# Experts of layer 1 take their tokens by one-hot products on the chip instead of gathers and transposes

## The chip, the cores and the metric

The kernel runs on one core of a Trainium2 chip. A run is one launch; its time is the device time in microseconds (us). The time of the kernel before is the median of three runs.

## The reference

Two layers of a hybrid backbone. Each layer mixes tokens (attention and a convolution), and then sends every token through the two best of 16 experts (a mixture of experts, MoE). Layer 0 does this for 512 tokens (256 of the context and 256 of the stream), layer 1 for the 256 of the stream. What matters here is the MoE; `t` has 1024 columns, an expert's inner width is 512, all in f32:

```python
combine = jnp.sum(jax.nn.one_hot(idx, N_EXPERTS) * wsel[..., None], axis=1)
y = jnp.zeros_like(t)
for e in range(N_EXPERTS):
    he = jax.nn.silu(t @ wg[e]) * (t @ wu[e])
    y = y + combine[:, e:e + 1] * (he @ wd[e])
```

`combine` is zero but for the two experts of a token, so a kernel need compute for each expert only the tokens that chose it. The product of a 0/1 matrix with the rows `t` that picks those tokens is exact in f32.

## The kernel before, in words

**The experts.** The expert's three matrices come as six tiles of 1 MB (two of `wg`, two of `wu`, two of `wd`) through a ring of 17 tiles. The SP queue issues them (L230), a tile as soon as one of the ring is free. All products of the experts run on TensorE (PE), in an order written out by hand in `moe`: in the iteration of expert e come the first halves of gate and up (`widen`, 32 matmuls), then the tokens of expert e+1 (`turn_tokens`), the transposes of the inner activations of expert e-1 (`turn_inner`), the second halves of gate and up (32 matmuls, for a wide expert 32 more of `widen_rest`), and the down product of e-1 (`down`, 48 matmuls, or `down_narrow`, 32). In layer 1 experts 0 to 5 are wide (96 places for tokens), 6 to 15 narrow (64 places).

**The tokens.** The normed and modulated rows `h` go to an array in device memory, `h2d`, 128 rows at a time (L841, on the SP queue). After routing, DVE builds a one-hot tile of the places of an expert, PE multiplies it with a table (`slots`, L1064: three columns that give the row numbers, three that give the weights), DVE turns the product into row numbers (`find`) and weights (`weigh`). With the row numbers POOL issues an indirect load (`gather`, L954) of 96 or 64 rows of 4 KB from `h2d`. The rows lie with tokens on the partitions, so PE transposes them in eight pieces (`turn_tokens`, L1214), and ACT and DVE copy the result `gp` into `tx`, the stationary operand of gate and up. The first two experts are found and gathered right after routing, each later one two iterations ahead.

**The opening of layer 1.** Around 700 us the order of the engines comes from generators that are woven together. `ada_row` makes the modulation rows: 64 products `ada` on PE, and then an add on DVE of a bias tile `ab`, which POOL's queue loads (L404); on POOL's queue these loads stand in program order between the loads (L2013) and the adds (L2039) of the filter spectra `K`. The list `held` holds the bias tiles that were asked for ahead; its entry 0 is that of the first row.

**The last experts.** Three experts at the end (TAIL) are added by products on the chip; the rest of a token's output is fetched by indirect loads into row buffers (`others_rows`).

Of the kernel before, what the change touches and what calls it, by code (L numbers as in the profile page):

```python
# [14 lines left out]
F32 = mybir.dt.float32  # L15
# [3 lines left out]
AF = mybir.ActivationFunctionType  # L19
ALU = mybir.AluOpType  # L20
# [4 lines left out]
P = 128  # L25
D = 1024
KD = 8
EPS = 1e-6
NEG = -1e30
NE = 16  # L30
# [219 lines left out]
def tile_hybrid_flow(ctx, tc, xin, rows, adab, w_ada, w_in_e, w_out_e, sinkb, rpb, w_in_o, w_out_o, hyw,  # L250
# [28 lines left out]
    def tpt(name):  # L279
        return btile([P, 4, P], "tp", name)  # L280
# [27 lines left out]
    def cc(name):  # L308
        o, n = CONST_AT[name]
        return cst[:, o : o + n]  # L310
# [510 lines left out]
    def g_h2(l, i, ti, a, h2, g2, sh2, rss, how):  # L821

        ss = small.tile([P, 1], F32, name=f"ssm{l}_{i}", tag="ss", bufs=4)
        S.activation(h2, xrow(ti), AF.Square, accum_out=ss)
        S.activation(rss[i], ss, AF.Sqrt, bias=epsc, scale=1.0 / D)
        yield
        V.reciprocal(rss[i], rss[i])

        def scale():
            V.scalar_tensor_tensor(h2, xrow(ti), rss[i], g2[:, a], op0=ALU.mult, op1=ALU.mult)  # L830

        if how in ("early", "first"):
            scale()
        yield
        if how == "late":
            scale()
        elif how == "aside":
            S.activation(h2, xrow(ti), AF.Copy, scale=rss[i])
            G.tensor_mul(h2, h2, g2[:, a])
        (V if how == "first" else G).tensor_add(h2, h2, sh2[:, a])  # L840
        SY.dma_start(h2d[l][i * P : (i + 1) * P, :], h2)  # L841
        yield
        yield

# [112 lines left out]
    def slot_table(l, pool):  # L957

        NT = 4 if l == 0 else 2
        tab = pool.tile([P, NT, NE, 6], BF, name=f"tab{l}")  # L960
        tb3 = tok_b.rearrange("p (i a) -> p i a", a=2)[:, 0:NT]
        for a in range(2):
            G.tensor_copy(tab[:, :, :, a], tb3[:, :, a : a + 1].to_broadcast([P, NT, NE]))
        G.tensor_copy(tab[:, :, :, 2:3], cc("far").unsqueeze(1).unsqueeze(2).to_broadcast([P, NT, NE, 1]))
        return tab

    def g_route(l, pool, s, r):
# [81 lines left out]
        def find(src, n, idst, hp):  # L1049

            f = hp.tile([P, NE], F32, name=f"idf{l}", tag="idf", bufs=1)[:, 0:n]
            V.reduce_sum(f, src[:, :, 0:3], axis=AX.X)
            newest["slots"] = V.tensor_scalar_add(idst, f, 4096.0).ins
# [4 lines left out]
        def slots(es, parts, idp=None):  # L1058
            idp = tpt(f"ids{l}_{es[0]}")[:, 0] if idp is None else idp
            for e in es:  # L1060
                for i in range(NT):
                    hot = one_hot(pool, lambda i: posm[:, i * NE + e : i * NE + e + 1], 0, i, 4, e >= WIDE[l])
                    o = 6 * (e - es[0])
                    T.matmul(idp[:, o + parts.start : o + parts.stop], hot, tab[:, i, e, parts], start=(i == 0), stop=(i == NT - 1))  # L1064
            return idp[:, 0 : 6 * len(es)].rearrange("p (e a) -> p e a", a=6)

        for e in range(2):
            find(slots([e], slice(0, 3)), 1, ids[:, e : e + 1], pool)
            gather(l, r["gts"][e][0 : SLOTS[l]], ids[0 : SLOTS[l], e : e + 1])
        if l == 0:  # L1070
# [47 lines left out]

        def group(e, idp):

            idp = slots([e], slice(0, 6), idp)
            at = slice(e, e + 1)

            def rest():
                find(idp, 1, ids[:, at], pool)
                weigh(idp, csl[:, at])

            return rest
# [39 lines left out]
            idp = slots([0, 1], slice(3, 6), idp)  # L1168
            return lambda: weigh(idp, csl[:, 0:2])

        r.update(eids=eids, weigh_first=weigh_first, posm=posm, ids=ids, csl=csl, group=group, rest=rest, find=find, weigh=weigh, one_hot=one_hot, pos=pos)
        yield

    def slots_hot(hot, at):
# [21 lines left out]
    def moe(l, r, gate5):  # L1196
# [7 lines left out]
        lp = lctx.__enter__()  # L1204
        def slots_of(e):
            return N if e < WIDE[l] else NARROW

        def turn_tokens(e):

# [145 lines left out]

        def others_rows(i):

            if i:
                t = W.pools["rest"][0].tile([P, 2, D], F32, name="yr0", tag="wt") if l == 0 else keep.tile([P, 2, D], F32, name="yr1", tag="xr0")
                d = [t[:, 0], t[:, 1]]  # L1360
            else:
                d = gts
            ex["rows", i] = combine_get(l, d, yb[0 : row_at(l, NE - TAIL[l]) + 1, :], r["rowi"], NT - 2 + i)

        def others_add(e, i):
# [36 lines left out]
            skip_runtime_bounds_check_because="a place's number is a sum over a one-hot row of the numbers of the experts")  # L1402
        lined = tc.manual_schedule(engines={T.engine})
        lined.__enter__()
        tx = turn_tokens(0)
        for e in range(NE + 1):
            if e:
                he = inner(e - 1, gu)
            if e < NE:
                gu = [acc(f"gu{l}_{e}_{a}") for a in range(1 + (e < WIDE[l]))]  # L1410
                cur, ups = tx, []
                widen(e, cur, gu, ups, 0)
            if e in (NE - 2, NE - 1):
                others_rows(NE - 1 - e)
            if e + 1 < NE:
                tx = turn_tokens(e + 1)
            if e:
                hx = turn_inner(e - 1, he)
            if e == NE - 2:
                others_slots()  # L1420
            if e == NE:
                for i in (1, 0):
                    others_take(i)
                others_open()
            if l and e == NE - 1:
                r["fg"] = W.pools["rest"][0].tile([P, 2, D], F32, name="fg", tag="wt")[:, 0]
                SY.dma_start(r["fg"], final_g[0].partition_broadcast(P))
            if e < NE:
                widen(e, cur, gu, ups, 1)
            if e:  # L1430
                (down if e <= WIDE[l] else down_narrow)(e - 1, hx)
            if e < WIDE[l]:
                widen_rest(cur, gu, ups)
            if e == NE - 1:
                W.limit = len(specs)
            if e == 1:
                with tc.issue_after(newest[V]):
                    r["rest"]()
# [569 lines left out]
    def hy_load(o):  # L2008
        K = [[None] * 2, [None] * 2]
        for ci in range(2):  # L2010
            for ft in range(2):
                K[ci][ft] = pool.tile([P, 512], F32, name=f"K{o}{ci}{ft}", tag="K", bufs=4)
                G.dma_start(K[ci][ft], kspec[o, ci, ft * P : ft * P + P, :])  # L2013
        return K
# [65 lines left out]
    def tail_side():  # L2080
# [4 lines left out]
        yield  # L2085
        yield from g_hyf(1, Ks[1])

    Ks = {0: hy_load(0)}
    weave(g_hyf(0, Ks[0]), chain(dense, ada_row(0)), 1.2)
    next_pools = {}  # L2090
# [31 lines left out]
    g2 = bcast(1, 4, pg, (1,))  # L2122
    sh2 = bcast(1, 3, pg, (1,))
    route1 = {}
    rows1 = m1.tile([P, 3, D], F32, name="rows1", tag="h2parts")
    G.memset(rows1[:, 0:2], 0.0)
    lgT = ypt("lg1")
    rss = [pb.tile([P, 1], F32, name=f"rsm1_{i}") for i in range(2)]
    rw = []
# [1 line left out]
    next(shares)  # L2131
    gate5 = bcast(1, 5, pb, (1,))
    h2x = keep.tile([P, 2, D], F32, name="h2x", tag="xr0")
    route1.update(gts=[rows1[:, 0], rows1[:, 1]], third=rows1[:, 2], tab=slot_table(1, pb))
    s1 = route_in(1, pg, pb, ob[1], shares, rw, [(2 + i, 1, 0) for i in range(2)], g2, sh2, rss, lgT, None, lambda i: h2x[:, i])
    routing = g_route(1, pb, s1, route1)
    next(routing)
# [65 lines left out]
```

## Time and profile before

| what | value |
|---|---|
| median of three runs | 1163.7 us (1157.68, 1163.7, 1164.82) |
| the profiled execution's own time | 1155.26 us |
| its span in the profile | 1153.1 us |
| PE busy | 1002.1 us, 87% of the span |
| DVE, ACT, POOL busy | 555.7, 382.2, 144.7 us |
| granted TensorE clock, mean of the span | 0.947 |
| moved by DMA | 328.88 MB, mean 285 GB/s |

The span is the stretch between the first and the last recorded instruction; 2.2 us of the execution's time lie around it. A clock of 1.00 is 2.4 GHz, 0.50 is 1.2 GHz. A busy PE is one that has a matmul in flight, and a time between the starts of two matmuls (their pitch) is what one costs in a row of them; the durations shown beside them overlap. "Landing" is the time from the issue of a transfer to its end.

### The profile page before, as it was taken

What the parts mean: (1) busy time and instruction counts of PE and PEld (TensorE: products, weight loads), DVE (VectorE), ACT (ScalarE), POOL (GpSimd) and SP (SyncE); (2) the same over time, 40 slices, a digit from 0 to 9 for tenths busy, and PEclk for the clock granted to TensorE, in tenths of its full rate; (3) what the DMA queues carried; (4) which work ended last, traced back from release to release, by engine and by line L of the source; (5) the groups of instructions that cost most, each with busy time, mean ns of one, the idle gap of its engine ahead of it and who ended that gap; (6) DMA issues with size and microseconds to landing.
All of it is one profiled execution on the core that took longest, in us unless ns stands there. A gap on an engine that the chain in (4) does not pass through costs nothing. (4 is left out here: it accounts for less than half of the span.)

```text
span 1153.1 us, 20964 instructions
## 1 busy us (share of the span) xinstructions
PE 1002.1 (87%) x8420; PEld 554.9 (48%) x8420; DVE 555.7 (48%) x1398; ACT 382.2 (33%) x855; POOL 144.7 (13%) x170
## 2 busy tenths in 40 slices
PE   5899999889893899999998677968893999998975
PEld 3587877566672333333332476767661333332222
DVE  7664655566447532332312683467656434321114
ACT  4545444342322233333221461443332333211111
POOL 2320002210205100000001102222012000000010
PEclk9999999999996899999999888998995999999997
DMA  8942122892957999999999835445288899999993
GB/s 332 420 142 75 37 74 71 311 331 79 404 222 272 320 323 388 405 398 395 402 400 420 342 130 229 147 151 190 91 354 300 280 368 413 403 383 409 418 418 162
DMA packets 55693, 328.88 MB, mean 285 GB/s; under 512 B 8546, under 2 KB 9026, under 8 KB 21474
## 3 DMA queue, kind: packets, MB, share of 16 engines
q1 hardware_dynamic: 41043, 285.93, 63.4%
q0 software_dynamic: 10096, 29.70, 7.8%
q10 hardware_dynamic: 4448, 11.81, 2.8%
q8 instruction: 70, 1.15, 0.4%
q14 instruction: 36, 0.29, 0.1%
HBM read 315.54 MB, written 16.06 MB: 288 GB/s over the span
## 5 line engine op out<-in xcount | busy, mean ns | idle before, releaser
L1234 PE MATMUL gu<-wt,tx 128*32 128x512 f32 x2560 | 305.5, 605 | 19.8 <-DMA wt<-in_moe_wu_dram 17.4
L1234 PEld LDWEIGHTS gu<-wt,tx 128*32 128x32 f32 x2560 | 81.8, 111 | 211.0 <-issue 170.9
L1234 PE MATMUL y<-wt,hx 128*32 128x512 f32 x1280 | 147.4, 593 | 0.0
L1234 PEld LDWEIGHTS y<-wt,hx 128*32 128x32 f32 x1280 | 43.8, 110 | 95.2 <-issue 93.2
L515 DVE TENSOR_TENSOR pair<-wt,pair 128x512 fp32r<-128x512 f32 x104 | 68.9, 711 | 16.6 <-ACT pair L512 16.4
L1223 ACT ACTIVATE tx<-gp 128x192 f32<-128x192 f32 (+1 forms) x64 | 19.3, 304 | 151.9 <-PE gp L1214 124.5
L1265 DVE TENSOR_TENSOR yo<-yo,y 32x512 f32<-32x512 f32 x32 | 21.8, 683 | 90.9 <-ACT yo L1263 90.6
L512 ACT ACTIVATE pair<-wt 128x512 fp32r<-128x512 f32 x104 | 58.4, 625 | 14.7 <-DMA wt<-in_w_in_o_dram 11.5
L1275 DVE TENSOR_TENSOR he<-he,up 96x512 f32<-96x512 f32 (+1 forms) x32 | 21.9, 685 | 82.4 <-ACT up L1274 81.9
L1224 DVE COPY tx<-gp 128x192 f32<-128x192 f32 (+1 forms) x64 | 20.3, 322 | 79.0 <-ACT tx L1223 78.5
L1270 ACT ACTIVATE he<-gu 96x512 f32<-96x512 f32 (+1 forms) x32 | 18.9, 591 | 116.2 <-PE gu L1234 116.2
L429 PE MATMUL ada<-wt,siluT 128*32 128x128 f32 x1536 | 51.3, 282 | 3.7 <-ACT pt L770 2.0
L429 PEld LDWEIGHTS ada<-wt,siluT 128*32 128x32 f32 x1536 | 41.5, 113 | 15.3 <-issue 8.1
L954 POOL DMA_INDIRECT gt<-h2d,ids x16 | 15.6, 976 | 202.8 <-DVE hot L1176 92.2
L1265 DVE TENSOR_TENSOR up<-up,gu 32x512 f32<-32x512 f32 x32 | 21.8, 683 | 36.3 <-ACT up L1263 36.0
L954 POOL DMA_INDIRECT rows<-h2d,ids x16 | 15.3, 958 | 182.7 <-DVE hot L1176 95.0
L768 PE MATMUL tp<-ident,pr 128*128 128x128 f32 x256 | 33.9, 275 | 0.0
L757 DVE TENSOR_SCALAR pr<-pr,ls 128x512 f32<-128x512 f32 (+1 forms) x80 | 32.5, 457 | 1.1
L741 ACT ACTIVATE pr<-sB,ng 128x512 f32<-128x512 f32 (+1 forms) x32 | 18.2, 578 | 41.9 <-DVE ng L734 36.2
L768 PEld LDWEIGHTS tp<-ident,pr 128*128 128x128 f32 x256 | 28.7, 141 | 4.5 <-issue 1.8
L520 PE MATMUL op<-pair,oh 128*128 128x512 f32 x64 | 27.5, 429 | 3.2 <-DVE pair L515 3.1
L519 PE MATMUL op<-pair,ol 128*128 128x512 f32 x64 | 28.0, 438 | 1.7 <-ACT pair L512 1.7
(482 smaller groups left out, 1906.9 us busy)
## 6 DMA issues: line engine op xcount, KB each, us to landing
wt<-in_moe_wg_dram SPq DMA_DIRECT2D x63, 1024.0 KB, 14.7
wt<-in_moe_wd_dram SPq DMA_DIRECT2D x63, 1024.0 KB, 15.4
wt<-in_moe_wu_dram SPq DMA_DIRECT2D x62, 1024.0 KB, 13.9
wt<-in_w_ada_dram SPq DMA_DIRECT2D x48, 1024.0 KB, 7.9
wt<-in_w_in_e_dram SPq DMA_DIRECT2D x9, 1024.0 KB, 15.8
wt<-in_w_in_o_dram SPq DMA_DIRECT2D x9, 1024.0 KB, 9.6
ybuf<-yo ACTq DMA_DIRECT2D x16, 384.0 KB, 7.2
bc<-mrow POOLq DMA_DIRECT2D x9, 512.0 KB, 11.2
```

What stands on the lines that cost most here:

```text
L429: T.matmul(ps[32 * j : 32 * j + 32, 0:P], siluT[:, k, :], w[:, k % 4, 128 * j : 128 * j + 128], start=(k == 0), stop=(k == KD - 1), tile_p ...
L512: newest["whi"] = S.activation(hi, w, AF.Copy).ins
L515: newest[eng] = eng.tensor_sub(lo, w, hi.bitcast(F32)).ins
L519: T.matmul(o, al, bh, start=first, stop=False)
L520: T.matmul(o, ah, bl, start=False, stop=False)
L757: V.tensor_scalar_mul(pr[:, h, at], pr[:, h, at], ls[:, h, j : j + 1])
L768: T.transpose(tp[:, kc], pr[:, h, kc * P : kc * P + P], ident)
L954: return G.indirect_dma_start(out=dst, out_offset=None, in_=h2d[l], in_offset=bass.IndirectOffsetOnAxis(ap=idx, axis=0), bounds_check=h2d[ ...
L1224: V.tensor_copy(tx[:, q * 4 + 2 : q * 4 + 4, 0:n], tp[:, 2:4, 0:n])
L1234: T.matmul(o[32 * c : 32 * c + 32], lhs, rhs, start=first, stop=last, tile_position=(0, 32 * c))
L1265: V.tensor_add(dst[q : q + 32], dst[q : q + 32], b[q : q + 32])
L1275: V.tensor_mul(he[0:n], he[0:n], up[0:n])
```

## The change

Four things change.

1. In layer 1 `pick_tokens` stands in the place of `turn_tokens`. `take_hot` builds on DVE two f32 one-hot tiles per expert (128 rows by 96 or 64 places). For each of eight column blocks of 128, PE multiplies the two tiles of rows `h2x`, which stay on the chip, with the two one-hot tiles: 16 f32 matmuls per expert, whose result is already turned. The searches for row numbers, the gathers and the transposes of layer 1 are gone; the product of places and table has three columns and only makes the weights, for expert e-1 (for the last expert too, in the last call).
2. `h2d` is written from POOL's queue in both layers, not from SP's.
3. The bias tile of the first modulation row of layer 1 is asked for before the K loads.
4. The row buffers of `others_rows` in layer 1 come from other pools, since `h2x` must live on, and `rows1` and its memset on POOL are gone.

```diff
--- before.py
+++ after.py
@@ -838,7 +838,7 @@
             S.activation(h2, xrow(ti), AF.Copy, scale=rss[i])
             G.tensor_mul(h2, h2, g2[:, a])
         (V if how == "first" else G).tensor_add(h2, h2, sh2[:, a])
-        SY.dma_start(h2d[l][i * P : (i + 1) * P, :], h2)
+        G.dma_start(h2d[l][i * P : (i + 1) * P, :], h2)
         yield
         yield
 
@@ -1064,7 +1064,14 @@
                     T.matmul(idp[:, o + parts.start : o + parts.stop], hot, tab[:, i, e, parts], start=(i == 0), stop=(i == NT - 1))
             return idp[:, 0 : 6 * len(es)].rearrange("p (e a) -> p e a", a=6)
 
-        for e in range(2):
+        def take_hot(e):
+
+            for i in range(NT):
+                V.tensor_scalar(r["hots"][e % 2][:, i, 0 : SLOTS[l]], cc("iota")[:, 0 : SLOTS[l]], posm[:, i * NE + e : i * NE + e + 1], None, op0=ALU.is_equal)
+
+        if l:
+            take_hot(0)
+        for e in range(2 - 2 * l):
             find(slots([e], slice(0, 3)), 1, ids[:, e : e + 1], pool)
             gather(l, r["gts"][e][0 : SLOTS[l]], ids[0 : SLOTS[l], e : e + 1])
         if l == 0:
@@ -1118,11 +1125,12 @@
 
         def group(e, idp):
 
-            idp = slots([e], slice(0, 6), idp)
+            idp = slots([e], slice(3 * l, 6), idp)
             at = slice(e, e + 1)
 
             def rest():
-                find(idp, 1, ids[:, at], pool)
+                if not l:
+                    find(idp, 1, ids[:, at], pool)
                 weigh(idp, csl[:, at])
 
             return rest
@@ -1168,7 +1176,7 @@
             idp = slots([0, 1], slice(3, 6), idp)
             return lambda: weigh(idp, csl[:, 0:2])
 
-        r.update(eids=eids, weigh_first=weigh_first, posm=posm, ids=ids, csl=csl, group=group, rest=rest, find=find, weigh=weigh, one_hot=one_hot, pos=pos)
+        r.update(eids=eids, weigh_first=weigh_first, posm=posm, ids=ids, csl=csl, group=group, rest=rest, take_hot=take_hot, find=find, weigh=weigh, one_hot=one_hot, pos=pos)
         yield
 
     def slots_hot(hot, at):
@@ -1204,6 +1212,27 @@
         lp = lctx.__enter__()
         def slots_of(e):
             return N if e < WIDE[l] else NARROW
+
+        def pick_tokens(e):
+
+            n = slots_of(e)
+            if e:
+                r["take_hot"](e)
+            hot = r["hots"][e % 2]
+            tx = lp.tile([P, KD, N], F32, name=f"tx{l}_{e}", tag="tx", bufs=2)
+            tps = [tpt(f"gp{l}_{e}_{q}") for q in range(2)]
+            for k in range(KD):
+                for i in range(NT):
+                    T.matmul(tps[k // 4][:, k % 4, 0:n], r["rows"][:, i, k * P : (k + 1) * P], hot[:, i, 0:n], start=(i == 0), stop=(i == NT - 1))
+            found = [r["group"](e - 1, tps[1][:, 3, n:P])] if e else []
+            if e == NE - 1:
+                found.append(r["group"](e, tps[0][:, 3, n:P]))
+            for q, tp in enumerate(tps):
+                S.activation(tx[:, q * 4 : q * 4 + 2, 0:n], tp[:, 0:2, 0:n], AF.Copy)
+                V.tensor_copy(tx[:, q * 4 + 2 : q * 4 + 4, 0:n], tp[:, 2:4, 0:n])
+            for f in found:
+                f()
+            return tx
 
         def turn_tokens(e):
 
@@ -1355,11 +1384,14 @@
 
         def others_rows(i):
 
-            if i:
-                t = W.pools["rest"][0].tile([P, 2, D], F32, name="yr0", tag="wt") if l == 0 else keep.tile([P, 2, D], F32, name="yr1", tag="xr0")
+            if l == 0 and i == 0:
+                d = gts
+            elif l and i:
+                t = wsp.tile([P, 4, 512], F32, name="yr1", tag="wt").rearrange("p (a b) n -> p a (b n)", a=2)
                 d = [t[:, 0], t[:, 1]]
             else:
-                d = gts
+                t = W.pools["rest" if i else "more"][0].tile([P, 2, D], F32, name=f"yr{l}{i}", tag="wt")
+                d = [t[:, 0], t[:, 1]]
             ex["rows", i] = combine_get(l, d, yb[0 : row_at(l, NE - TAIL[l]) + 1, :], r["rowi"], NT - 2 + i)
 
         def others_add(e, i):
@@ -1402,7 +1434,8 @@
             skip_runtime_bounds_check_because="a place's number is a sum over a one-hot row of the numbers of the experts")
         lined = tc.manual_schedule(engines={T.engine})
         lined.__enter__()
-        tx = turn_tokens(0)
+        tokens = pick_tokens if l else turn_tokens
+        tx = tokens(0)
         for e in range(NE + 1):
             if e:
                 he = inner(e - 1, gu)
@@ -1413,7 +1446,7 @@
             if e in (NE - 2, NE - 1):
                 others_rows(NE - 1 - e)
             if e + 1 < NE:
-                tx = turn_tokens(e + 1)
+                tx = tokens(e + 1)
             if e:
                 hx = turn_inner(e - 1, he)
             if e == NE - 2:
@@ -2085,6 +2118,7 @@
         yield
         yield from g_hyf(1, Ks[1])
 
+    held[0] = ada_bias(*order_c[0][0:2], po)
     Ks = {0: hy_load(0)}
     weave(g_hyf(0, Ks[0]), chain(dense, ada_row(0)), 1.2)
     next_pools = {}
@@ -2122,8 +2156,7 @@
     g2 = bcast(1, 4, pg, (1,))
     sh2 = bcast(1, 3, pg, (1,))
     route1 = {}
-    rows1 = m1.tile([P, 3, D], F32, name="rows1", tag="h2parts")
-    G.memset(rows1[:, 0:2], 0.0)
+    hots = m1.tile([P, 4, P], F32, name="hots1", tag="h2parts")
     lgT = ypt("lg1")
     rss = [pb.tile([P, 1], F32, name=f"rsm1_{i}") for i in range(2)]
     rw = []
@@ -2131,7 +2164,7 @@
     next(shares)
     gate5 = bcast(1, 5, pb, (1,))
     h2x = keep.tile([P, 2, D], F32, name="h2x", tag="xr0")
-    route1.update(gts=[rows1[:, 0], rows1[:, 1]], third=rows1[:, 2], tab=slot_table(1, pb))
+    route1.update(gts=None, rows=h2x, hots=[hots[:, 2 * b : 2 * b + 2] for b in range(2)], tab=slot_table(1, pb))
     s1 = route_in(1, pg, pb, ob[1], shares, rw, [(2 + i, 1, 0) for i in range(2)], g2, sh2, rss, lgT, None, lambda i: h2x[:, i])
     routing = g_route(1, pb, s1, route1)
     next(routing)
```

**TensorE at the start of layer 1's experts.** Before (`ids` are the products that give row numbers, `gp` the transposes, `gu` gate and up):

```order
L1064 LDWEIGHTS hot_8491
L1064 MATMUL ids_1_8490<-tab_8274,hot_8491 128x3
L1064 LDWEIGHTS hot_8494
L1064 MATMUL ids_1_8490<-tab_8274,hot_8494 128x3
L1214 MATMUL gp_0_0_8602<-ident,rows_8250 128x96 x4
L1214 MATMUL gp_0_1_8603<-ident,rows_8250 128x96 x4
L1234 MATMUL gu_0_0_8616<-wt,tx_0_8601 32x512 x16
L1214 MATMUL gp_1_0_8637<-ident,rows_8250 128x96 x4
L1214 MATMUL gp_1_1_8638<-ident,rows_8250 128x96 x4
```

With the change (`hots` are the f32 one-hot tiles; one row here is a matmul in f32, which the trace records as two instructions):

```order
L1226 MATMUL gp_0_0_8577<-hots_8250,h2x 128x96 x8
L1226 MATMUL gp_0_1_8578<-hots_8250,h2x 128x96 x8
L1263 MATMUL gu_0_0_8599<-wt,tx_0_8576 32x512 x16
L1226 MATMUL gp_1_0_8622<-hots_8250,h2x 128x96 x8
L1226 MATMUL gp_1_1_8623<-hots_8250,h2x 128x96 x8
L1064 LDWEIGHTS hot_8640
L1064 MATMUL gp_1_1_8623<-tab_8273,hot_8640 128x3
L1064 LDWEIGHTS hot_8643
L1064 MATMUL gp_1_1_8623<-tab_8273,hot_8643 128x3
L1263 MATMUL gu_0_0_8599<-wt,tx_0_8576 32x512 x16
```

The products with the table ahead of the first transposes are gone, and the first tokens come from 16 products instead of 8 transposes; 16 more stand ahead of the second half of expert 0.

**POOL's queue at the opening of layer 1.** Before (`hyk`, `K` and `ab` are loads, the TENSOR_TENSOR rows are POOL's own adds):

```order
L1946 DMA hyk_6842<-in_hyc_dram 128x1024
L2013 DMA K_6844<-kspec 128x512
L2013 DMA K_6846<-kspec 128x512
L2013 DMA K_6848<-kspec 128x512
L2013 DMA K_6850<-kspec 128x512
L2039 TENSOR_TENSOR K_6844<-K_6844,zt_6852 128x512
L2039 TENSOR_TENSOR K_6848<-K_6848,zt_6852 128x512
L2039 TENSOR_TENSOR K_6846<-K_6846,zt_6852 128x512
L2039 TENSOR_TENSOR K_6850<-K_6850,zt_6852 128x512
L404 DMA ab_2_0_6962<-in_adab_dram 128x256
L404 DMA ab_4_0_6964<-in_adab_dram 128x256
L404 DMA ab_4_1_6965<-in_adab_dram 128x256
```

With the change:

```order
L1979 DMA hyk_6842<-in_hyc_dram 128x1024
L404 DMA ab_2_0_6844<-in_adab_dram 128x256
L2046 DMA K_6846<-kspec 128x512
L2046 DMA K_6848<-kspec 128x512
L2046 DMA K_6850<-kspec 128x512
L2046 DMA K_6852<-kspec 128x512
L2072 TENSOR_TENSOR K_6846<-K_6846,zt_6854 128x512
L2072 TENSOR_TENSOR K_6850<-K_6850,zt_6854 128x512
L2072 TENSOR_TENSOR K_6848<-K_6848,zt_6854 128x512
L2072 TENSOR_TENSOR K_6852<-K_6852,zt_6854 128x512
L404 DMA ab_4_0_6964<-in_adab_dram 128x256
L404 DMA ab_4_1_6965<-in_adab_dram 128x256
```

The first of the three `ab` loads stands ahead of the four K loads and of the adds that wait for them.

**POOL's queue ahead of layer 0's experts.** Before (L840 makes the rows `h`, L954 are the first two gathers):

```order
L840 TENSOR_TENSOR h_0_0_3155<-h_0_0_3155,bc_3_3123 128x1024
L840 TENSOR_TENSOR h_0_1_3156<-h_0_1_3156,bc_3_3123 128x1024
L840 TENSOR_TENSOR h_0_2_3157<-h_0_2_3157,bc_3_3123 128x1024
L954 DMA gt_0_3109<-h2d_73,ids_3511 96x1024
L954 DMA gt_1_3110<-h2d_73,ids_3511 96x1024
```

With the change:

```order
L840 TENSOR_TENSOR h_0_0_3155<-h_0_0_3155,bc_3_3123 128x1024
L841 DMA h2d_73<-h_0_0_3155 128x1024
L840 TENSOR_TENSOR h_0_1_3156<-h_0_1_3156,bc_3_3123 128x1024
L841 DMA h2d_73<-h_0_1_3156 128x1024
L840 TENSOR_TENSOR h_0_2_3157<-h_0_2_3157,bc_3_3123 128x1024
L841 DMA h2d_73<-h_0_2_3157 128x1024
L841 DMA h2d_73<-h_0_3_3158 128x1024
L954 DMA gt_0_3109<-h2d_73,ids_3511 96x1024
L954 DMA gt_1_3110<-h2d_73,ids_3511 96x1024
```

Four writes of `h2d` stand between POOL's adds and ahead of the gathers that read `h2d`; from SP's queue, where they stood ahead of weight loads, they are gone.

## Rows read from the trace of the kernel before

**Rows 1.** Windows: us busy of PE, PEld, DVE, ACT, POOL (instructions), clock, DMA share, GB/s.

```profile
1050.00:1100.00 50.00, 43.72 (x352) 13.83 (x354) 7.45 (x22) 5.99 (x15) 1.89 (x2) 1.00 1.01 417
```

**Rows 2.** Timeline of PE: start, duration, instructions [idle before <-releaser]; later half of the experts.

```profile
1035.29 3.62 PE L1234 MATMUL gu<-wt,tx 128*32 128x512 f32 x32
...
1101.05 0.71 PE L1214 MATMUL gp<-ident,rows 64*128 64x64 f32 x8
...
1111.48 1.03 PE L1234 MATMUL gu<-wt,tx 128*32 128x512 f32 x4
1114.62 3.63 PE L1234 MATMUL gu<-wt,tx 128*32 128x512 f32 x28 [2.11 <-DMA wt<-in_moe_wu_dram]
...
1131.75 0.40 PE L1282 MATMUL hp<-ident,he 64*128 64x64 f32 x3
```

**Rows 3.** Timeline of PE: the token transposes in a wide and a narrow iteration.

```profile
923.51 0.88 PE L1214 MATMUL gp<-ident,rows 96*128 96x96 f32 x8
924.23 0.20 PE L1064 MATMUL gp<-tab,hot 128*128 128x6 bf16 x2
...
1015.63 0.71 PE L1214 MATMUL gp<-ident,rows 64*128 64x64 f32 x8
1016.27 0.21 PE L1064 MATMUL gp<-tab,hot 128*128 128x6 bf16 x2
...
1027.24 0.71 PE L1214 MATMUL gp<-ident,rows 64*128 64x64 f32 x8
```

**Rows 4.** Timeline of PE and DVE at the start of layer 1's experts.

```profile
878.77 0.48 DVE L1043 TENSOR_SCALAR hot<-cst,posm 128x128 bf16<-128x128 f32 x2
...
888.39 1.51 PE L1214 MATMUL gp<-ident,rows 96*128 96x96 f32 x8 [7.87 <-DMA rows<-h2d,ids]
...
896.25 10.51 PE L1234 MATMUL gu<-wt,tx 128*32 128x512 f32 x96
```

**Rows 5.** Timeline of PE: short f32 matmuls with 128x128 weights.

```profile
726.33 0.95 PE L1955 MATMUL msk<-cst,sqk 128*128 128x2 f32 x8
727.13 1.97 PE L2048 MATMUL yc<-hyk,K 128*128 128x256 f32 x8
728.94 0.60 PE L654 MATMUL kvct<-ident,kvcr 128*128 128x128 f32 x4
...
733.94 1.05 PE L1965 MATMUL sck<-ident,widek 128*128 128x128 f32 x8
734.75 0.36 PE L519 MATMUL qc<-hh,pair 128*128 128x256 f32 x1
```

**Rows 6.** Timeline of PEld, the weight loads of the last of these.

```profile
733.82 0.98 PEld L1965 LDWEIGHTS sck<-ident,widek 128*128 128x128 f32 x8
```

**Rows 7.** Timeline of PE at the opening of layer 1.

```profile
701.72 1.95 PE L429 MATMUL ada<-wt,siluT 128*32 128x128 f32 x64 [0.42 <-issue]
709.71 0.79 PE L519 MATMUL kvck<-hh,pair 128*128 128x512 f32 x1 [6.03 <-DVE ab L434]
...
714.13 0.39 PE L520 MATMUL kvck<-hl,pair 128*128 128x512 f32 x1
```

**Rows 8.** Timeline of POOL at the opening of layer 1.

```profile
669.62 1.60 POOL L2013 DMA_DIRECT2D K<-kspec  x3 [14.56 <-DVE xs L1194]
...
702.65 1.63 POOL L404 DMA_DIRECT2D ab<-in_adab_dram  x3
```

**Rows 9.** Timeline of POOL and PE around layer 0's first gather.

```profile
349.89 8.91 POOL L840 TENSOR_TENSOR h<-h,bc 128x1024 f32<-128x1024 f32 x3
367.28 1.12 POOL L954 DMA_INDIRECT gt<-h2d,ids  x1 [8.48 <-DVE hot L1043]
...
377.26 1.51 PE L1214 MATMUL gp<-ident,gt 96*128 96x96 f32 x8 [9.73 <-DMA gt<-h2d,ids]
```

**Rows 10.** DMA issues: queue, count, KB each, median us; then POOL-issued `bc` alone.

```profile
h2d<-h SPq DMA_DIRECT2D x4, 512.0 KB, 6.4
...
DMA to landing us min/median/max: 3.3/9.9/19.6
```

## The prediction

> **What bounds the kernel now.** I read the windows first, to see in which stretch of layer 1 what is late. From 1050 to 1100 us PE is busy 43.72 of 50 us while the DMA engines are full (share 1.01, 417 GB/s) [rows 1]: there the stream of weights sets the pace. The timeline of PE shows the same from within: the idle time ahead of gate and up ends with the landing of a weight tile, 2.11 us in the case shown [rows 2]. The stretch from the first gate product of expert 10 (1035.29) to the end of the down product of expert 14 (1131.75) lasts 96.46 us [rows 2]. A narrow iteration that waits for nothing takes 11.61 us (1015.63 to 1027.24) [rows 3]. Without waits the stretch would be four of these (46.4), expert 14's with the extra turning work (3.5 for the first half of gate and up, then 1101.05 to 1111.48, 13.9) and expert 15's without tokens and table (10.8), together 71.1 us. So about **25.3 us of waits for weights** lie in it. Before it, PE itself sets the pace: its iterations follow one another with no idle time shown [rows 3].
>
> Two other places are read in the timeline because the change touches them: the start of layer 1's experts, where PE waits 7.87 us for the first gather [rows 4], and its opening, where PE waits 6.03 us for an add on DVE, which waits for the bias tile `ab` [rows 7].
>
> **Part 1, the price of a product.** Per expert, 8 transposes go and 16 f32 matmuls come, which the trace records as 32 instructions with a 128x128 weight load each. The nearest row is `sck`, also f32 with 128x128 weights: 0.81 us from its start to the next product's, for 8 instructions, 0.101 each. `msk` has 2 moving columns instead of 128 and costs the same, 0.80 for 8 [rows 5]; so here the weight load sets the pitch, and 96 or 64 columns give nothing back. The loads of `sck` take 0.98 us for 8, 0.1225 each [rows 6], an upper bound, since the last one's own latency is in it. The transposes, with a load each, run at 0.09 (0.72 for 8) wide and 0.08 (0.64 for 8) narrow [rows 3], the lower bound. I take **0.105**, close to `sck`, whose kind and weights are the same: 3.36 us per expert, 2.64 more than the transposes of a wide expert and 2.72 more than those of a narrow one. The table products that remain stay as they are (0.20); two late experts get one that had none, 0.4 together. The one-hots are two DVE instructions of some 0.24 us each per expert [rows 4]; DVE is busy 7.45 of 50 us there [rows 1] and PE needs them an iteration later, so they cost nothing; without that cover they would cost 0.5 us per expert.
>
> **Part 2, the start of the experts.** The one-hot of expert 0 is ready where the search's one-hot was, 878.77 + 0.48 = 879.25 [rows 4]. The 32 instructions begin at the slow clock: at the opening of layer 1, after a wait, the matmuls kept the longer duration (0.79, later 0.39) for 4.4 us [rows 7]. At 0.21 each, 21 instructions fill 4.4 us, the other 11 take 1.2: done at 884.8. Then 3.5 us for the first half of gate and up, 3.4 for the tokens of expert 1, 0.2 for the table: the second half starts at 891.9 instead of 896.25 [rows 4], **-4.4 us**. The other 14 experts cost 4 x 2.64 + 10 x 2.72 = **+37.8**, with the tables +38.2.
>
> **Part 3, what the waits give back.** A narrow iteration then takes 14.3 us on PE. A narrow expert's 6.29 MB of weights and 0.26 MB of outputs take 15.7 us at 417 GB/s [rows 1]: still more, by 1.4 us, 14 us over ten experts. But the wide iterations (144 matmuls at 10.51/96 = 0.109, 15.8 [rows 4], with the products over 19) leave the stream 3 us each to fill the ring, and 17 tiles are 42.7 us of lead at that rate; the gathers' 1216 rows of 4 KB, 5 MB, are gone too. The lead outlasts the deficit, so all of the 25.3 us goes: PE's new work fills time in which PE waited. Next late would be PE itself. Layer 1's experts: -4.4 + 38.2 - 25.3 = **+8.5 us**; as a formula 448 x pitch - 38.5.
>
> **Part 4, `ab` early.** POOL issued `ab` at 702.65, behind the K adds, and PE stood from the end of `ada` (703.67) until 709.71 [rows 7, 8]. Asked for before the K loads, which wait for DVE until 669.62 in any case [rows 8], `ab` lies ready 30 us early and the K loads lose one issue, 0.53 us (1.60 for 3). The wait of 6.03 goes, and of the 4.4 us in which the matmuls after it ran at the slow clock half, 2.2: **-8**; if the next operand is late instead, between 0 and -6.
>
> **Part 5, `h2d` from POOL's queue.** In layer 1 nobody reads it before the rare overflow pass: nothing. In layer 0 the first gather reads it; PE waits 9.73 us for it [rows 9]. POOL's adds end at 349.89 + 8.91 = 358.80; four issues at 0.53 put the last write at 360.9, against the gather's 367.28, which the row numbers set: 6.4 us are there. From SP the write landed in 6.4 [rows 10], so I take 0. Bounds: POOL-issued transfers of the same size landed between 3.3 and 19.6 us [rows 10], so up to +13.2; and SP, no longer blocked behind `h`, can load weights earlier, which empties the DMA engines for the gather, down to -3.
>
> **Sum:** +8.5 - 8 + 0 = +0.5 us, on the profiled execution's 1155.3 (span 1153.1 and 2.2 around it): 1155.8. That execution is 8.4 below the median, 1163.7, which gives 1164.2. The three runs spread over 7 us; waits for the stream are where an execution can lose more than this one did, and they go. I take 3 us off for that, a judgement: **1161 us**, no change. A measurement here can tell about 1% from no change, 1152.1 to 1175.3.
>
> **Rivals.**
> *Columns, not loads, set the pitch (faster).* `yc` takes 1.81 us for 8 instructions of 256 columns, 0.226 each [rows 5], or 0.085 for 96 and 0.057 for 64 columns. If the loads hide, an expert costs 2.71 wide, 1.81 narrow: 1.99 and 1.17 more than before, the start gains 1.3 more: -5.7 + 8.0 + 11.7 + 0.4 - 25.3 - 8 = -18.9, about **1142 us**. PE would then need 12.8 us per narrow expert, the stream would lose 29 us of its lead of 42.7, and would just not bind. For it: PE loads while it multiplies, PEld 13.83 us beside PE's 43.72 [rows 1]. Against it: `msk` with 2 columns. The Trainium skill (TensorE: Matmul & The Clock Gate, Back-to-back issue gap) gives 81 ns for a load with a 128-column matmul in a long stream; by that the sum would be 448 x 0.081 - 38.5 - 8 = -10.2 and the time about 1150. The trace shows 101 ns for `sck` in a series of only 8.
>
> *The first gather of layer 0 waits for `h2d` (slower).* It decides as soon as a write from POOL's queue lands later than 6.4 us after its issue. At the 9.9 median of rows of that size it costs 3.5 us, at the 19.6 maximum 13.2 [rows 10]: **1174 us**. For it: those rows. Against it: SP's 6.4, and fewer weights in flight at that time. The Trainium skill (DMA: Bandwidth & Descriptors, Issuing engine by pattern) sends plain stores to the sync engine and calls its path generally faster, a rule that speaks against this move; no run so far shows the same write on both queues.
>
> *`ab` early gains nothing.* The products after `ada` may wait for something else that ends at the same time: +8, **1169 us**. Against it: PE's wait names the DVE add alone [rows 7].
>
> **Chances.** Forecast 0.62 (own range 1149 to 1172: pitch 0.08 to 0.1225 is -11 to +8, `ab` up to +3, `h2d` -3 to +3.5, the basis 3 either way); columns 0.15; `h2d` 0.13; `ab` 0.10. Faster by over 1%: columns 0.14 and the forecast's low end 0.10, 0.24. Slower by over 1%: 0.06 of `h2d`, 0.03 of `ab`, 0.05 of the forecast, 0.14. Within: 0.62. Range for 8 in 10: 1145 to 1175, which leaves out the lower part of the columns' case and the ends.
>
> **What would show it.** Right: `gp` at 3.2 to 3.5 us per expert from its start to the next instruction; no idle time on PE for weights after 1040; the second half of expert 0 some 4 us earlier relative to the routing; no wait ahead of `kvck`. Wrong: `gp` in narrow iterations shorter than in wide ones (columns count); waits for `wu` tiles again before the end (the lead was too small); the first gather of layer 0 issued late or landing late; the wait ahead of `kvck` ended by another releaser; or a clock under 1.00 in the products, which would double their price.

## The result, and the profile after

Over 20 runs of each kernel the change takes 1166.99 us (1162.4 to 1171.54) and the kernel before 1160.0 (1155.76 to 1166.84): ratio **1.0055**, 95% interval 1.0039 to 1.0072, some 6.4 us slower. The forecast was 1161 and no change; the time lies in its range, its small gain has the wrong sign. The profiled execution of after took 1162.69 us, 7.4 more than that of before, so the two traces can be compared stage by stage.

Two windows of after, the second that of [rows 1] (us busy of PE, PEld, DVE, ACT, POOL, then clock, DMA share, GB/s):

```profile
950.00:1000.00 50.00, 50.00 (x466) 23.00 (x462) 17.97 (x42) 12.19 (x25) 0.00 (x0) 1.00 0.87 347
1050.00:1100.00 50.00, 50.00 (x460) 24.90 (x453) 10.53 (x32) 6.32 (x16) 0.00 (x0) 1.00 0.83 326
```

In both PE is full and the DMA engines no longer are: the bound has changed sides, as forecast. The timeline of PE in after, a wide and a narrow iteration and the end, against [rows 2, 3]:

```profile
894.65 3.81 PE L1226 MATMUL gp<-hots,h2x 128*128 128x96 f32 x32
898.30 0.19 PE L1064 MATMUL gp<-tab,hot 128*128 128x3 bf16 x2
...
1009.65 3.79 PE L1226 MATMUL gp<-hots,h2x 128*128 128x64 f32 x32
1013.27 0.19 PE L1064 MATMUL gp<-tab,hot 128*128 128x3 bf16 x2
...
1119.20 4.51 PE L1263 MATMUL gu<-wt,tx 128*32 128x512 f32 x32
...
1137.29 1.92 PE L1263 MATMUL y<-wt,hx 128*32 128x512 f32 x16 [1.04 <-SPq L1478]
```

The 32 instructions cost 3.65 us with 96 columns and 3.62 with 64, 0.114 and 0.113 each: columns give nothing back, and the price is 8% above the 0.105 that was taken. Near the end one wait remains (1.04, ahead of the second half of a down product, whose tiles SP had issued only at 1118.82), and 32 gate and up matmuls ran 0.9 us longer, behind three short waits (granted clock 0.79 from 1115.44 to 1123.50).

The start of the experts in after, against [rows 4]:

```profile
870.82 0.45 DVE L1070 TENSOR_SCALAR hots<-cst,posm 128x96 f32<-128x96 f32 x2
871.24 5.70 PE L1226 MATMUL gp<-hots,h2x 128*128 128x96 f32 x32 [0.68 <-DVE hots L1070]
876.87 3.64 PE L1263 MATMUL gu<-wt,tx 128*32 128x512 f32 x32
880.44 3.81 PE L1226 MATMUL gp<-hots,h2x 128*128 128x96 f32 x32
884.09 0.19 PE L1064 MATMUL gp<-tab,hot 128*128 128x3 bf16 x2
884.21 10.51 PE L1263 MATMUL gu<-wt,tx 128*32 128x512 f32 x96
```

The wait of 7.87 us for the first gather is gone: the products begin as soon as the one-hots are there. The first 32 instructions take 5.63 us (granted clock 0.64), the next 32 take 3.65.

The opening of layer 1 in after, POOL, PE and ACT, against [rows 7, 8]:

```profile
666.08 0.58 POOL L404 DMA_DIRECT2D ab<-in_adab_dram  x1 [13.94 <-DVE yg L1200]
697.43 1.95 PE L429 MATMUL ada<-wt,siluT 128*32 128x128 f32 x64 [0.42 <-issue]
699.32 0.50 PE L519 MATMUL kvck<-hh,pair 128*128 128x512 f32 x1
710.05 0.50 PE L519 MATMUL kvcv<-hh,pair 128*128 128x512 f32 x1 [3.23 <-ACT rawk L2008]
711.64 0.63 PE L519 MATMUL kvcv<-hh,pair 128*128 128x512 f32 x1
708.36 1.15 ACT L512 ACTIVATE pair<-wt 128x512 fp32r<-128x512 f32 x2 [11.59 <-DMA wt<-in_w_in_o_dram]
709.42 0.58 ACT L2008 ACTIVATE rawk<-kvck 128x512 f32<-128x512 f32 x1
```

The wait ahead of `kvck` is gone, and a new one stands ahead of `kvcv`: PE needs the bank that ACT empties (`rawk`), and in ACT's queue that copy stands behind the split (`pair`) of a weight tile that lands only at 708.36. From 711.64 the matmuls behind the new wait run at the longer duration again, 0.63 (granted clock 0.50 from there to 714.20). ACT in before, at the same place:

```profile
712.51 1.15 ACT L512 ACTIVATE pair<-wt 128x512 fp32r<-128x512 f32 x2 [11.45 <-DMA wt<-in_w_in_o_dram]
717.55 0.60 ACT L1975 ACTIVATE rawk<-kvck 128x512 f32<-128x512 f32 x1 [3.89 <-PE kvck L521]
```

There too ACT stood at that tile, but PE came later still, so `rawk` waited for PE. SP issued the tile 0.8 us ahead of the end of `ada` in both traces (702.85 and 698.56), and ACT had it 8.8 and 9.0 us behind that end: the early bias tile did not move it.

Layer 0's first gather in after: SP, POOL, DVE (the row numbers), PE, and the writes' landing, against [rows 9, 10]; then SP and DVE in before:

```profile
346.65 0.33 SPq L230 DMA_DIRECT2D wt<-in_moe_wg_dram  x1
347.08 1.35 SPq L230 DMA_DIRECT2D wt<-in_moe_wd_dram  x2
360.72 0.55 POOL L841 DMA_DIRECT2D h2d<-h  x1 [0.53 <-DVE lgr L903]
366.88 0.15 DVE L1053 TENSOR_SCALAR ids<-idf 128x1 int32<-128x1 f32 x1
369.02 1.02 POOL L954 DMA_INDIRECT gt<-h2d,ids  x1 [7.75 <-DVE places L1090]
373.24 1.51 PE L1243 MATMUL gp<-ident,gt 96*128 96x96 f32 x8 [5.18 <-DMA gt<-h2d,ids]
h2d<-h POOLq DMA_DIRECT2D x4, 512.0 KB, 7.3
```

```profile
360.33 0.44 SPq L230 DMA_DIRECT2D wt<-in_moe_wg_dram  x1
360.86 2.94 SPq L230 DMA_DIRECT2D wt<-in_moe_wd_dram  x2
366.35 0.15 DVE L1053 TENSOR_SCALAR ids<-idf 128x1 int32<-128x1 f32 x1
```

SP no longer waits for `h`; three weight tiles go out at 346 to 348 instead of 360 to 363, and the gather takes 4.2 us from its issue to PE's start instead of 10.0 (mean DMA share in that stretch 0.53 instead of 1.02). The write itself lands later than from SP, 7.3 against 6.4, and this shows: the gather is issued 1.99 us behind its row numbers (367.03) instead of 0.78. The profile names a DVE step as the releaser; but in the kernels that write `h2d` from POOL the gather starts 1.6 to 7.0 us behind its row numbers, in those that write it from SP 0.4 to 0.8, and here it starts 1.0 us behind the end of the last write. So I put these 1.2 us down to the write.

Where the time went, from marks on PE that all traces have (us): A, the first `pos` product of layer 0's routing, to the first token transposes; B, the end of `ada` to the first `qc` product; C, the first `pos` product of layer 1's routing to the last eight `last` products, which end the experts.

| kernel | first `pos` at | A | B | C |
|---|---|---|---|---|
| before | 364.15 | 13.11 | 25.63 | 261.93 |
| after | 364.69 | 8.55 | 22.63 | 277.28 |
| ab_only | 371.31 | 13.11 | 22.45 | 264.96 |
| h2d_only | 362.25 | 8.61 | 25.09 | 264.28 |
| ab_h2d | 370.02 | 9.68 | 24.53 | 261.41 |
| prod_only | 367.58 | 12.68 | 25.67 | 278.06 |
| mixed | 366.97 | 9.51 | 20.90 | 269.43 |
| mixed_late2 | 369.78 | 9.25 | 21.07 | 257.45 |
| start2 | 367.40 | 9.27 | 22.43 | 259.36 |
| sp_held | 364.82 | 13.49 | 24.54 | 267.36 |
| bf16c | 363.68 | 9.00 | 20.81 | 259.79 |

Before to after: A -4.6, B -3.0, C +15.3, all else together some -0.3. The first column moves by 9 us between kernels that are nearly the same up to there, and the profiled executions with a small value there (362 to 365) lie mostly below the median of their kernel: much of the scatter of the runs seems to arise before layer 0's routing. Each row is one execution.

### The profile page after: what moved, and what is told of

The parts are those of the page before. It is cut to its first block, busy times and chain, and to the rows that moved or that the text cites. A ratio compares the mean times of both kernels' runs of the same rounds, so it can differ in the third digit from the quotient of the medians.

```text
span 1160.9 us, 21650 instructions
## 1 busy us (share of the span) xinstructions
PE 1037.2 (89%) x8800; PEld 598.0 (52%) x8800; DVE 559.5 (48%) x1395; ACT 382.4 (33%) x855; POOL 129.1 (11%) x159
## 5 line engine op out<-in xcount | busy, mean ns | idle before, releaser
L1263 PE MATMUL gu<-wt,tx 128*32 128x512 f32 x2560 | 296.8, 605 | 6.2 <-DMA wt<-in_moe_wu_dram 6.2
L1263 PE MATMUL y<-wt,hx 128*32 128x512 f32 x1280 | 144.6, 593 | 1.0 <-SPq L1478 1.0
L1226 PEld LDWEIGHTS gp<-hots,h2x 128*128 128x128 f32 x512 | 60.3, 197 | 13.3 <-issue 13.3
L1226 PE MATMUL gp<-hots,h2x 128*128 128x64 f32 (+1 forms) x512 | 62.6, 282 | 0.7 <-DVE hots L1070 0.7
L1231 ACT ACTIVATE tx<-gp 128x128 f32<-128x128 f32 (+1 forms) x32 | 9.4, 297 | 114.1 <-PE gp L1226 79.0
L954 POOL DMA_INDIRECT gt<-h2d,ids x16 | 15.5, 969 | 197.9 <-DVE hot L1184 92.2
L1190 POOL DMA_INDIRECT yr<-ybuf,rowi x6 | 5.8, 963 | 277.6 <-DMA wt<-in_moe_wg_dram 251.0
L1232 DVE COPY tx<-gp 128x128 f32<-128x128 f32 (+1 forms) x32 | 10.0, 314 | 53.5 <-ACT tx L1231 53.5
```

The lines of the kernel that those rows point to most:

```text
L954: return G.indirect_dma_start(out=dst, out_offset=None, in_=h2d[l], in_offset=bass.IndirectOffsetOnAxis(ap=idx, axis=0), bounds_check=h2d[ ...
L1226: T.matmul(tps[k // 4][:, k % 4, 0:n], r["rows"][:, i, k * P : (k + 1) * P], hot[:, i, 0:n], start=(i == 0), stop=(i == NT - 1))
L1263: T.matmul(o[32 * c : 32 * c + 32], lhs, rhs, start=first, stop=last, tile_position=(0, 32 * c))
```

## The experiments

All ran against the kernel before, with 6 to 12 runs each. The first four take the change apart.

**ab_only, h2d_only, ab_h2d, prod_only.**

```diff
 ab_only, ab_h2d:    +    held[0] = ada_bias(*order_c[0][0:2], po)
 h2d_only, ab_h2d:   -        SY.dma_start(h2d[l][i * P : (i + 1) * P, :], h2)
                     +        G.dma_start(h2d[l][i * P : (i + 1) * P, :], h2)
 prod_only:          the change without these two edits
```

> The kernel before with the early bias tile alone. Theory A (parts add up, as the two profiles show them stage by stage): the wait of 6.03 us ahead of kvck goes, but the next weight tile of the opening lands only some 4 us earlier and PE waits some 3 us ahead of kvcv instead; 4 us faster than before (-3 to -5). Theory B (the term as predicted): no new wait, 8 us faster. Theory C (the end of layer 1's experts is set by the weight stream, which swallows an earlier start): under 1.5 us faster.

> The kernel before with the h2d writes on POOL's queue alone. Theory A: SP, no longer blocked behind the rows h, loads three weight tiles some 14 us earlier, the first gather of layer 0 finds emptier DMA engines and PE starts 4 us earlier at the first transposes: 4 us faster (-2.5 to -5). Theory B (as predicted): 0. Theory C (stream swallows it): under 1.5 us faster.

> The kernel before with both moves and the gathers and transposes of layer 1 kept. Theory A: the two gains add, 8 us faster than before (-6 to -9.5), the fastest kernel so far, with the waits for weights late in layer 1 still there. Theory B: 8 us faster too, but by another split. Theory C: under 3 us faster, the waits for weights late in layer 1 longer by what the start won.

> The change without the early bias tile and with h2d on SP's queue: products of layer 1 alone. Theory A: layer 1's experts cost 15 us more (products at 0.1135 us an instruction, 3.65 per expert), 15 us slower than before (+12 to +17). Theory B (as predicted, 0.105 an instruction): 8.5 us slower. Theory C (the products alone are even, the slowdown comes from the moves): within 3 us of before.

Measured: ab_only 0.9973 (0.9951 to 0.9996), -3 us; h2d_only 0.9937 (0.9915 to 0.9960), -7 us; ab_h2d **0.9915** (0.9883 to 0.9946), -10 us; prod_only **1.0127** (1.0099 to 1.0155), +15 us. Theory A holds: the parts add up within their intervals (-3 - 7 + 15, the change measured +6.4), and in the medians an earlier start is not swallowed later, though C is 3.0 and 2.4 us longer in the single traces of ab_only and h2d_only. The term as predicted for `ab` (-8) lies outside its interval, as does the 0 for `h2d`. Of h2d_only's 7 us its trace shows 4.5 in A; where the rest arises is open.

**sp_held: is it SP's freedom?**

```diff
-        SY.dma_start(h2d[l][i * P : (i + 1) * P, :], h2)
+        G.dma_start(h2d[l][i * P : (i + 1) * P, :], h2)
+        SY.dma_start(stub[4 * l + i : 4 * l + i + 1, 0:256], h2[0:1, 0:256])
```

> The kernel before with h2d written from POOL's queue, and in its old place on SP's queue a stub, a write of 1 KB from each tile of the rows h to an unused array, so that SP waits for h as before. Theory A (the gain of the move is that SP is no longer blocked and three weight tiles are loaded ahead of the gather): the gain goes, within 2 us of before, and PE waits more than 8 us for the first gather again. Theory D (the write from POOL's queue lands sooner, or the gather behind it on the same queue runs faster): the gain of 7 us stays, and PE waits some 5 us.

Measured: 1.0016 (0.9994 to 1.0038). The timeline of SP, POOL and PE in sp_held:

```profile
352.94 7.87 SPq L843 DMA_DIRECT2D stub<-h  x4
360.89 0.36 SPq L230 DMA_DIRECT2D wt<-in_moe_wg_dram  x1
374.17 1.02 POOL L956 DMA_INDIRECT gt<-h2d,ids  x1 [12.76 <-DMA h2d<-h]
378.31 1.51 PE L1216 MATMUL gp<-ident,gt 96*128 96x96 f32 x8 [10.12 <-DMA gt<-h2d,ids]
```

With SP held, the gain is gone, though POOL writes `h2d`: it came from the weight tiles that left early, and theory D is out. But the 10.12 us are not the wait of before. Once issued, the gather took 4.14 us; it was issued 7.0 us behind its row numbers (367.15), because POOL's last write, now beside the weight tiles of 361, landed 12.4 us after its issue. This is the prediction's rival in which the first gather waits for `h2d`; it costs 1.2 us in after and some 6 here. In layer 1 of sp_held the first gather is late too (PE waits 11.88 instead of 7.87).

The Trainium skill (DMA: Bandwidth & Descriptors, Issuing engine by pattern) sends plain stores to the sync engine; the landing times agree (7.3 against 6.4). What stood behind the store in SP's queue was worth more.

**bf16, bf16b, bf16c: is the pitch the f32 weight load?** The rows as three bf16 parts whose sum is the f32 row (against the change; `...` marks lines left out):

```diff
-                    T.matmul(tps[k // 4][:, k % 4, 0:n], r["rows"][:, i, k * P : (k + 1) * P], hot[:, i, 0:n], start=(i == 0), stop=(i == NT - 1))
+                    parts = [r["rows"]] if e < 2 else r["rows16"]
+                    for c, rw in enumerate(parts):
+                        T.matmul(tps[k // 4][:, k % 4, 0:n], rw[:, i, k * P : (k + 1) * P], hot[:, i, 0:n], start=(i == 0 and c == 0), stop=(i == NT - 1 and c == len(parts) - 1))
+            if e == 0:
+                for i in range(NT):
...
+                    S.activation(h1, h, AF.Copy)
+                    G.tensor_sub(t, h, h1)
+                    S.activation(h2, t, AF.Copy)
+                    G.tensor_sub(h3, t, h2)
 bf16b: e < 3, the split behind the tokens of expert 1 (e == 1) in the program
 bf16c: as bf16b, and S.activation(h1, h, AF.Copy, scale=one), one = tx[:, 6, 0:1] * 0 + 1
```

> The changed kernel, but from expert 2 on the rows are three bf16 parts, whose sum is the f32 row, and the one-hots bf16: 48 matmuls of one bf16 instruction per expert instead of 16 of two f32 instructions; the parts are made on ACT and POOL during expert 0. Theory A (the pitch is the f32 weight load, 0.1135; bf16 loads with few columns ran at 0.03 to 0.05 in the routing): 2.0 to 2.4 us per expert instead of 3.65, some 18 us faster than the change, 11 us faster than before (1145 to 1153). Theory E (the pitch is a cost of any instruction with a new 128x128 load, whatever its type): 5.4 us per expert, 25 us slower than the change.

> As bf16, but the split of the rows is put off until the tokens of expert 1 are copied, and expert 2 takes f32 products too. Theory A (the 6.4 us that routing took longer in bf16 is DVE stalled beside POOL's subtractions, which then ran during routing): routing takes its old time again, DVE is stalled later where nothing waits; 4 to 6 us faster than bf16, 1147 to 1151. Theory I (DVE's long step in bf16 had another cause, such as the place of the tiles in memory): as slow as bf16, 1154, plus 1.6 for expert 2.

> As bf16b, whose split did not move in the trace; now the split reads a factor of one that DVE makes from the tokens of expert 1, so that it can't start earlier. Theory A (DVE is stalled by POOL's subtractions, whenever they run): routing as short as in the change (the wait of PE for it 6.5 us instead of 12.98), 6 us faster than bf16b, 1148 to 1152; DVE's stall stands after 890 and costs nothing. Theory I (the 6.67 us step of DVE has another cause): PE still waits 12.98, 1156.

Measured: bf16 0.9955 (0.9930 to 0.9981), bf16b 0.9970 (0.9947 to 0.9993), bf16c **0.9911** (0.9876 to 0.9947). The timeline of PE in bf16, the first and the last rows of a wide and a narrow expert's products:

```profile
905.05 0.26 PE L1230 MATMUL gp<-hots 128*128 128x96 bf16 x2
...
907.10 0.19 PE L1064 MATMUL gp<-tab,hot 128*128 128x3 bf16 x2
...
977.66 0.23 PE L1230 MATMUL gp<-hots 128*128 128x64 bf16 x2
...
979.07 0.19 PE L1064 MATMUL gp<-tab,hot 128*128 128x3 bf16 x2
```

48 matmuls cost 2.05 us wide and 1.41 narrow, 0.043 and 0.029 each: with bf16 loads the columns set the pitch, with f32 loads the load does, at 0.113. The Trainium skill (TensorE: Matmul & The Clock Gate, Weight-path perf modes — Fast Weight Load (FWL) and DoubleRow) says that the fast weight load is on for 128 weights that are not FP32; these numbers agree.

bf16 gained less than expected, because routing took 6.5 us longer. The timeline of DVE and POOL in bf16 shows why:

```profile
871.31 6.67 DVE L991 TENSOR_TENSOR oh<-oh,cst 128x32 f32<-128x32 f32 x1
871.65 4.21 POOL L1244 TENSOR_TENSOR hrest<-h2x,hots 128x1024 f32<-128x1024 f32 x2
875.81 2.11 POOL L1246 TENSOR_TENSOR rows<-hrest,hots 128x1024 bf16<-128x1024 f32 x1
878.02 0.18 DVE L993 TENSOR_REDUCE rmax<-oh 128x8 f32<-128x32 f32 x1
882.29 2.36 POOL L1246 TENSOR_TENSOR rows<-hrest,hots 128x1024 bf16<-128x1024 f32 x1 [4.37 <-ACT hots L1245]
882.60 2.13 DVE L1070 TENSOR_SCALAR hots<-cst,posm 128x96 bf16<-128x96 f32 x1
```

The same step, and PE's wait for the routing, in bf16c:

```profile
866.80 0.19 DVE L991 TENSOR_TENSOR oh<-oh,cst 128x32 f32<-128x32 f32 x1
869.45 0.20 PE L1024 MATMUL pos<-A,bfc 128*128 128x16 bf16 x1 [6.44 <-DVE A L1017]
```

A DVE step that took 0.19 us in before ended with POOL's subtractions. In bf16b the program order alone did not move the split, and the same step took 6.67 again; its time is the one that Theory I gave, but as the split had not moved it decides nothing. In bf16c the split ran behind expert 1's tokens, the step took 0.19, PE's wait for routing fell from 12.98 to 6.44, and the kernel gained what was expected. The Trainium skill (SBUF — State Buffer, Who interferes with whom) has a rule for this: a DVE instruction with two SBUF inputs contends with a GpSimd instruction that reads SBUF. The trace agrees.

**mixed, mixed_late, mixed_late2, start2: what is a product worth where?** Both moves in all; f32 products for some experts, gathers for the others (the central lines, against the change):

```diff
# mixed: experts below PICK[l], with PICK = (0, 8); the others by `picks`:
+        return l == 1 and (e < 2 or e >= 10)       # mixed_late, mixed_late2
+        return l == 1 and e < 2                    # start2
-        tokens = pick_tokens if l else turn_tokens
+        tokens = lambda e: (pick_tokens if picks(l, e) else turn_tokens)(e)
 mixed_late2, start2, in pick_tokens, against mixed_late's:
-            if e < 2:
-                found.append(r["group"](e + 2, tps[0][:, 2, n:P]))
+            if e == 1:
+                found += [r["group"](2 + q, tps[q][:, 2, n:P]) for q in range(2)]
```

> Both moves as in the change; experts 0 to 7 take their tokens by f32 products, 8 to 15 by gathers and transposes as before. Theory A (PE's extra time is free as long as PE would wait for weights; products save the gathers' bytes and 4 us at the start): the waits for weights late in layer 1 are nearly gone, some 6 us faster than both moves alone, 16 us faster than before (1141 to 1148). Theory F (products cost their full time wherever they stand): 8 x 2.95 less 4, 19 us slower than both moves alone, 1170.

> As mixed, but the products stand at the two places where PE waits: experts 0 and 1 (the start) and 10 to 15 (the weight-bound stretch); 2 to 9 take gathers and transposes. Theory G (a product costs nothing where PE waits for weights and its full 2.9 us where PE sets the pace; mixed had most of them in the wrong place): 4 us saved at the start and 3.8 us of gather traffic in the weight-bound stretch, 6 to 8 us faster than both moves alone, 14 to 18 us faster than before (1140 to 1146). Theory H (in the weight-bound stretch the stream is not slowed by the gathers, only the order of arrival counts): no faster than both moves alone, about 1150.

> As mixed_late, but the search for the rows of expert 2 moves from the tokens of expert 0 to those of expert 1: in mixed_late it stood ahead of expert 0's gate and up on PE and waited 3.48 us for the table. Theory G (a product is free only where PE waits): the start now gains its 4 us, and the clock does not fall in between; 5 to 6 us faster than mixed_late, 1145 to 1149, some 12 us faster than before and 4 faster than both moves alone. Theory H (what the start gains, the weight stream takes back): as mixed_late, 1153.

> Both moves, and products for experts 0 and 1 alone; 2 to 15 take gathers and transposes. Theory G (the start is worth its 4 us by itself, and the products of 10 to 15 add what their gathers cost the stream, some 2 to 4): between both moves alone and mixed_late2, 3 to 4 us faster than both moves, 1147 to 1150. Theory H (an earlier start is taken back by the weight stream, whose late waits grow by what was won): as both moves alone, 1151 to 1152, with 4 us more of waits for weights late in layer 1.

Measured: mixed 0.9998 (0.9977 to 1.0018), mixed_late 0.9945 (0.9924 to 0.9965), mixed_late2 **0.9895** (0.9867 to 0.9922, 1147.16 us), start2 **0.9890** (0.9853 to 0.9928, 1148.69 us). Mixed missed theory A, and fell short of theory F: its C is 8.0 us longer than with both moves alone. Most of its products stood in the wide iterations, where PE sets the pace, and only part of their price came back later, when PE waited 7.7 us for gate and up weights instead of 10.8. Its windows:

```profile
900.00:950.00 50.00, 50.00 (x466) 22.21 (x469) 19.79 (x65) 12.41 (x25) 0.00 (x0) 1.00 0.72 283
1050.00:1100.00 50.00, 46.33 (x400) 16.00 (x398) 10.03 (x32) 7.63 (x19) 2.80 (x3) 1.00 1.01 407
```

The DMA share early is 0.72, and late, at 1.01, PE waits again. PE in mixed_late:

```profile
883.37 0.19 PE L1064 MATMUL gp<-tab,hot 128*128 128x6 bf16 x2 [3.48 <-DVE tab L1122]
883.99 5.98 PE L1271 MATMUL gu<-wt,tx 128*32 128x512 f32 x32 [0.43 <-ACT tx L1236]
```

Mixed_late gained 6 us where theory G had 14 to 18: the search for expert 2 stood ahead of the first gate and up, PE waited 3.48 us there for the table, and gate and up took 5.98 us behind the wait instead of 3.64. Its C, 262.83, was no shorter than with both moves alone. In mixed_late2 that wait is gone and the products stand where PE waits; no wait for gate and up weights is left, and C is 4.0 us shorter than with both moves alone. start2 gets half of that in its trace (C 2.1 shorter) and the same in its time; the intervals don't tell the two apart, so what the late products add is open. They overlap that of ab_h2d too (0.9883 to 0.9946), so what the early products add to both moves rests on single traces. Both beat the kernel before and the change.

## Why the prediction was right or wrong

- **Right: which side binds.** The waits for weights went, the lead of the ring outlasted the narrow experts, and PE's work filled the time. As "Part 3" put it, 25.3 us should come back; in C behind the start, +19.4 us were measured (896.25 to 1140.14 before, 884.21 to 1147.54 after), against 41.5 of products and 0.4 of tables: 22.5 came back. The 2.8 missing are the new wait of 1.04 and, near the end, 0.9 of slower matmuls and 0.8 more in the turning work ahead of them.
- **Right: the start.** -4.4 forecast; -4.1 measured from the first `pos` product to the second half of expert 0 (18.04 to 13.95). The first 32 instructions took 5.63 us, forecast 5.6.
- **Wrong in size: the price of a product.** "I take 0.105": it is 0.1135, between `sck`'s pitch and its loads' 0.1225 [rows 5, 6]. 14 experts make +3.7 us of that. That a series of only 8 hides one load in its edges would fit, but no run shows it; I leaned on the lower row. The rival of the columns fell with the same rows (3.65 us wide, 3.62 narrow). The 81 ns of the Trainium skill (TensorE: Matmul & The Clock Gate, Back-to-back issue gap) were further off than 0.105. The Trainium skill (TensorE: Matmul & The Clock Gate, LDWEIGHTS (loading the stationary operand)) puts a load's ns at its columns over 1.2, by which I estimate 107 ns, 6% below the measured pitch.
- **Wrong: the 8 us of `ab`.** The step that failed is to book the whole wait of 6.03 and the 2.2 of slow matmuls behind it as gain; that the next operand may be late instead was priced as a bound, but not followed up in the trace of before. B fell by 3.0 and the edit alone gained 3 us. In place of the old wait stands one of 3.23 ahead of `kvcv`, again with slow matmuls behind it. [rows 7] name only the wait that ended last; ACT stood at the next weight tile 11.45 us at that place in before too, until 712.51, hidden behind the wait for `ab`. B lies 1.1 to 4.8 under that of before in the kernels that have the edit, and 0 to 1.1 under it in the others. That the late tile causes the new wait is read from the traces (it stands in after, ab_only and ab_h2d); no experiment moved the tile by itself. So the rival "`ab` early gains nothing" was right for 5 of the 8 us.
- **Wrong: 0 for `h2d`.** Both bounds came, and they did not cancel. Emptier DMA engines shortened the gather by 5.8 us, more than the 3 that I allowed; the write from POOL landed late by 1.2. Together they are the 4.6 in A.
- **Wrong, and lucky: 3 us off for scatter.** The median of 20 runs lies 4.7 above the profiled execution in before and 4.3 in after, so nothing went. But the median of three had put that distance at 8.4; the 3 us taken off for a reason that did not hold made up for most of that, by luck.

On the profiled executions the forecast was +0.5 and the measurement +7.4: `ab` +5, pitch +3.7, waits not given back +2.8, `h2d` -4.6. The first two had errors of one sign, and the sum, close to zero, took its sign from them. That the time lies in the range, which is 30 us wide, says little for the terms.

## What to carry to other kernels

Price a short f32 matmul by its weight load, and count two loads each; if an operand is 0/1 or exact in parts, bf16 parts can be cheaper though they are more instructions. Extra work on an engine is free only in the stretch where that engine waits, so place it there, stretch by stretch. A store that waits for its data holds up the loads behind it in its queue, so look at what stands there before choosing the queue. Before booking a whole wait as gain, find what the other engines stand at while it lasts.

## What the runs showed of the hardware that was not expected

A two-input DVE step of 128x32 elements took 6.67 us instead of 0.19 while POOL ran three two-input subtractions of 128x1024 (bf16, bf16b); a one-hot step, with one tile and one number per row as its operands, took 2.13 instead of 0.26 beside the fourth (bf16). The last 512 KB write from POOL's queue landed in 7.3 us in after and in 12.4 in sp_held, where three weight tiles of 1 MB went out beside it. An f32 product with 64 columns cost as much as with 96 (3.62 and 3.65 us for 32), a bf16 one scaled with them (1.41 and 2.05 for 48).
